# Layer 0 of a two-layer encoder trunk: inverse square roots of a head pair by one Heron step and reciprocals, with the intermediate rows in PSUM

## The chip, the cores and the metric

One core of a Trainium2 chip runs the whole step as one program. The metric is the device time of one execution in microseconds (us). TensorE (PE) multiplies matrices into PSUM, VectorE (DVE) and ScalarE (ACT) work on SBUF and PSUM, GpSimd (POOL) on SBUF, and SyncE (SP) issues nearly all DMAs. Each engine takes its instructions in the order of its own queue; semaphores hold an instruction back until what it needs is there.

## The reference

One inference step on a prompt of 512 tokens and a sample of 32. Layer 0 is an RWKV-7 time mixer, layer 1 a differential attention; each has one input projection, four heads of attention to a memory, a gate, and an output projection. What matters here are two normalizations in layer 0's mixer, both by head of 64 columns:

```python
kk = k * k_k
kk = kk / jnp.maximum(jnp.linalg.norm(kk, axis=-1, keepdims=True), 1e-12)
...
mean = jnp.mean(y, axis=-1, keepdims=True)
var = jnp.mean(jnp.square(y - mean), axis=-1, keepdims=True)
y = (y - mean) * lax.rsqrt(var + GN_EPS) * ln_w + ln_b
```

Both need an inverse square root: one per token and head of the squared norm of the keys, one of the variance of the outputs.

## The kernel before

The 512 + 32 = 544 tokens lie in one matrix. Layer 0 works through its 24 heads in 12 pairs. Three strands are woven together, in an order that a table of numbers (`PLAN`, line 49, with `FILL0` to `FILL3` ahead of the loop and `TAIL` behind it, lines 83 to 89) and a small planner in `layer0` write out:

- the main stream: projections with weight blocks of 128 columns. PE makes a block in two halves of 272 tokens, each of 24 products into one PSUM buffer `ps_g`, as the operands are split in a high and a low part (`hh`, `hl` and `whi`, `wlo`). DVE makes `wlo` of the next block (line 106 is the helper through which every instruction of PE, DVE, ACT and SP goes, so nearly all rows of the profile say L106).
- the chain of a pair: the state `SB` is carried from chunk to chunk by small products into `ps_c`, which DVE and ACT take up.
- steps of other pairs: the preparation of pairs to come (`rw_prep`, "prep"), and the end of the pair before (`rw_finish`, "fin").

PSUM is handed out in pools. The pool `psg` (line 2167) has three buffers of one bank each, given out in turn; all half products of the main stream take theirs there, and a buffer is written again only when the last reader of what was in it is done. At the end of layer 0 the output projection starts (`w_out`, line 1382). For a block of its first kind it takes two buffers at once, one for each half of the tokens, and alternates between them.

The inverse square roots of a pair are made by one call. `rw_prep` of one pair puts the 16 squared norms of each partition into the first columns of the row tile `q20` (line 669), and `rw_finish` of an earlier pair puts 10 variances behind them (line 1103). The entry "rsq" of the table (line 67, in `TAIL`, and three calls ahead of the loop) then calls `rsqrt` on all 26 columns (line 1468), which leaves the results in `r20`. `rw_finish` multiplies the pair's outputs `yt` by ten of them (line 1105), after which PE transposes `yt` into `ps_y`; `rw_prep` copies the other 16 into `rr` (line 699). There are 16 calls. In the profile both `q20` and `r20` are called `q`, and the scratch row `nt`.

`rsqrt` (line 131) is the integer estimate of an inverse square root, one Newton step and one step of higher order: eight DVE instructions, each on 128 partitions of 26 numbers in SBUF, each using the result of the one ahead of it. Other places in the kernel use it too, and are not touched.

On POOL, `rw_invert` (lines 861 and 863) makes the triangular inverses of a later pair with up to 62 small instructions, at the same time.

Of the kernel before, what the change touches and what calls it, by code (L numbers as in the profile page):

```python
# [9 lines left out]
F32 = mybir.dt.float32  # L10
F32R = mybir.dt.float32r
BF16 = mybir.dt.bfloat16
I32 = mybir.dt.int32
AF = mybir.ActivationFunctionType
ALU = mybir.AluOpType
AX = mybir.AxisListType

P = 128
# [90 lines left out]
class Trunk:  # L109
# [21 lines left out]
    def rsqrt(self, y, x, pool, tag):  # L131

        nc = self.nc
        t = pool.tile(list(y.shape), F32, tag=tag, name=tag)
        f = 0.375 ** 0.2
        self.ve.tensor_scalar(y.bitcast(I32), x.bitcast(I32), -0.5, float(0x5F3759DF), ALU.mult, ALU.add)
        self.ve.scalar_tensor_tensor(t[:], y, -0.5 * f, y, ALU.mult, ALU.mult)
        self.ve.tensor_tensor(t[:], t[:], x, ALU.mult)
        self.ve.scalar_tensor_tensor(y, t[:], 1.5 * f, y, ALU.add, ALU.mult)
        self.ve.tensor_tensor(t[:], y, y, ALU.mult)  # L140
        self.ve.tensor_tensor(t[:], t[:], x, ALU.mult)
        self.ve.scalar_tensor_tensor(t[:], t[:], -10.0 / 3.0 * f ** 2, t[:], ALU.add, ALU.mult)
        self.ve.scalar_tensor_tensor(y, t[:], 5.0 * f ** 4, y, ALU.add, ALU.mult)

    def params(self, p, name, rows, queue=None):

        t = p.tile([P, P], F32, name=name)
        r0 = 0
        for src, n in rows:
            (queue or self.se).dma_start(t[r0 : r0 + n, :], src)  # L150
            r0 += n
        return t, r0
# [1281 lines left out]
    def layer0(self, mem):  # L1434
        nc, o = self.nc, self.o
        w = self.a["rw_in"][0]
# [4 lines left out]
        with ExitStack() as ctx:  # L1441
# [23 lines left out]
            def go(kind, pr):  # L1465

                if kind == "rsq":
                    self.rsqrt(self.r20[:], self.q20[:], self.rk0, "nt")
                elif 0 <= pr < NPAIR:
                    if kind in ("inv", "back", "at"):  # L1470
                        {"inv": self.rw_invert, "back": self.rw_back, "at": self.rw_at}[kind](sts[pr])
                        return
                    if (kind, pr) not in run:
                        it = run[kind, pr] = self.rw_prep(sts[pr], rkv[pr]) if kind == "prep" else make[kind](sts[pr])
                        next(it)
                    next(run[kind, pr], None)
# [96 lines left out]
            for k, n in enumerate(FILL0):  # L1573
                go("prep", 0)
                if k == 3:
                    go("rsq", 0)
                if k == 26:
                    go("inv", 0)
                fill(n)
# [94 lines left out]
        with ExitStack() as ctx:  # L1674
# [67 lines left out]
            for i in range(5):  # L1742
                n = P if i < 4 else TS
# [493 lines left out]
```

## Time and profile before

| | |
|---|---|
| median of 3 runs | 1403.26 us (1402.6 to 1403.94) |
| the profiled execution | 1402.28 us, of which the span from the first to the last instruction is 1400.5 us |
| granted TensorE clock | 0.996 |
| PE busy | 1361.5 us of the span |
| DVE busy | 934.6 us |
| ACT busy | 828.6 us |
| POOL busy | 371.7 us |

How to read it: times are us from the start of the span unless marked ns. A row of the timeline gives start, duration, engine, line, operation, what is written and read (`out<-in`), and the shape; in brackets the idle time ahead of it and who ended it. A row of the waits gives who waited for whom, the time in total, how often, and the longest. PE counts a matmul as busy from its start to its end, though matmuls overlap: products of 272 columns start 0.125 us apart while each is shown with 0.29 us.

### The profile page before, as it was taken

What the parts mean: (1) busy time and instruction counts of PE and PEld (TensorE: products, weight loads), DVE (VectorE), ACT (ScalarE), POOL (GpSimd) and SP (SyncE); (2) the same over time, 40 slices, a digit from 0 to 9 for tenths busy, and PEclk for the clock granted to TensorE, in tenths of its full rate; (3) what the DMA queues carried; (4) which work ended last, traced back from release to release, by engine and by line L of the source; (5) the groups of instructions that cost most, each with busy time, mean ns of one, the idle gap of its engine ahead of it and who ended that gap; (6) DMA issues with size and microseconds to landing.
All of it is one profiled execution on the core that took longest, in us unless ns stands there. A gap on an engine that the chain in (4) does not pass through costs nothing.

```text
span 1400.5 us, 31939 instructions
## 1 busy us (share of the span) xinstructions
PE 1361.5 (97%) x11893; PEld 1296.7 (93%) x11893; DVE 934.6 (67%) x2345; ACT 828.6 (59%) x2304; POOL 371.7 (27%) x841
## 2 busy tenths in 40 slices
PE   8999999999999999999999999999999999999997
PEld 6988899999998998897899999999999999999997
DVE  5765777787877787676753476676467756767443
ACT  5756677767776777565543366664466546665222
POOL 2136567555865576520000040000000001001000
PEclk9999999999999999999999999999999999999999
DMA  7543222332233222342474473333333322332321
GB/s 224 155 118 80 49 57 76 84 96 62 67 82 99 61 77 73 87 131 64 121 206 118 120 218 108 92 92 93 101 92 94 104 73 84 97 106 84 91 76 72
DMA packets 264036, 139.45 MB, mean 100 GB/s; under 512 B 57721, under 2 KB 252802, under 8 KB 263882
## 3 DMA queue, kind: packets, MB, share of 16 engines
q1 hardware_dynamic: 263818, 137.41, 34.9%
q8 instruction: 94, 1.54, 0.5%
q14 instruction: 60, 0.49, 0.1%
q10 hardware_dynamic: 64, 0.02, 0.0%
HBM read 111.12 MB, written 22.91 MB: 96 GB/s over the span
## 4 chain that ended last, share of the span: by engine, by line
PE 81%; DVE 8%; ACT 3%; issue 2%; POOL 2%; DMA 2%; SPq 1%; DVEq 0%; ACTq 0%; POOLq 0%
PE ps_g L106 57%; PE ps_c L106 4%; PE ps_s L106 2%; PE ps_o L106 2%; PE ps_at L106 2%; DVE wlo L106 1%; PE ps_v L106 1%; SPq L106 1%; PE ps_mm L106 1%; PE ps_mo L106 1%; POOL tm L861 1%; PE ps_aT L106 1%; PE ps_yc L106 1%; POOL u L863 1%; PE ps_kv L106 1%
## 5 line engine op out<-in xcount | busy, mean ns | idle before, releaser
L106 PE MATMUL ps_g<-hh,whi 128*128 128x272 f32 x1808 | 541.0, 300 | 0.4 <-DVE memk L106 0.2
L106 PE MATMUL ps_g<-hh,wlo 128*128 128x272 f32 x1808 | 536.0, 297 | 1.6 <-DVE wlo L106 1.6
L106 PE MATMUL ps_g<-hl,whi 128*128 128x272 f32 x1808 | 532.1, 295 | 0.6 <-DVE hl L106 0.3
L106 PEld LDWEIGHTS ps_g<-hh,wlo 128*128 128x128 f32 x1808 | 341.7, 189 | 6.3 <-DVE wlo L106 2.3
L106 PEld LDWEIGHTS ps_g<-hh,whi 128*128 128x128 f32 x1808 | 341.9, 189 | 5.8 <-DVE og L106 0.6
L106 PEld LDWEIGHTS ps_g<-hl,whi 128*128 128x128 f32 x1808 | 341.8, 189 | 4.6 <-DVE hl L106 1.3
L106 DVE TENSOR_TENSOR wlo<-raw,whi 128x512 fp32r<-128x512 f32 x314 | 220.9, 714 | 123.0 <-ACT whi L106 119.2
L106 ACT CAST whi<-raw 128x512 fp32r<-128x512 f32 x314 | 189.1, 619 | 109.5 <-PE ps_g L106 61.4
L861 POOL TENSOR_TENSOR tm<-u,m 102x84 f32<-102x84 f32 (+23 forms) x341 | 143.7, 421 | 165.5 <-DMA m<-sc 139.7
L863 POOL TENSOR_TENSOR u<-u,tm 102x84 f32<-102x84 f32 (+23 forms) x341 | 148.3, 435 | 26.6
L106 PE MATMUL ps_g<-hi,whi 128*128 128x272 f32 x512 | 148.9, 291 | 0.0
L106 PE MATMUL ps_g<-hi,wlo 128*128 128x272 f32 x512 | 147.5, 288 | 0.5 <-DVE wlo L106 0.5
L106 PE MATMUL ps_g<-lo,whi 128*128 128x272 f32 x512 | 147.4, 288 | 0.0
L1333 POOL TENSOR_TENSOR lo<-og,hi 128x544 fp32r<-128x544 f32 x8 | 13.2, 1652 | 359.7 <-ACT hi L106 359.2
L106 PEld LDWEIGHTS ps_g<-hi,wlo 128*128 128x128 f32 x512 | 96.4, 188 | 0.8 <-DVE wlo L106 0.7
L106 PEld LDWEIGHTS ps_g<-hi,whi 128*128 128x128 f32 x512 | 96.4, 188 | 0.0
L106 PEld LDWEIGHTS ps_g<-lo,whi 128*128 128x128 f32 x512 | 96.4, 188 | 0.0
L106 ACT ACTIVATE pt<-ps_s,snm 128x128 f32<-128x128 f32 (+3 forms) x96 | 51.0, 532 | 41.7 <-DVE snm L106 41.6
L106 DVE SCALAR_TENSOR_TENSOR SB<-ps_c,dl,sd 64x64 f32<-64x64 f32 x168 | 47.4, 282 | 40.9 <-PE ps_c L106 37.7
L1754 POOL TENSOR_TENSOR hl<-hn,hh 128x544 fp32r<-128x544 f32 x8 | 12.5, 1567 | 211.3 <-ACT hh L106 211.2
L106 ACT ACTIVATE sg<-ps_g 128x272 f32<-128x272 f32 x64 | 25.3, 396 | 57.6 <-PE ps_g L106 53.0
L106 ACT COPY sv<-ps_c 64x64 f32<-64x64 f32 x192 | 39.5, 206 | 33.3 <-PE ps_c L106 31.2
(402 smaller groups left out, 2578.3 us busy)
## 6 DMA issues: line engine op xcount, KB each, us to landing
raw<-in_rw_in_dram SPq DMA_DIRECT2D x114, 256.0 KB
raw<-in_df_in_dram SPq DMA_DIRECT2D x112, 256.0 KB
raw<-in_w_out_dram SPq DMA_DIRECT2D x64, 256.0 KB
oscr<-sg SPq DMA_DIRECT2D x16, 272.0 KB
lo<-oscr SPq DMA_DIRECT2D x16, 272.0 KB
m<-sc SPq DMA_DIRECT2D x33, 128.0 KB
raw<-in_w_mem_v_dram SPq DMA_DIRECT2D x16, 256.0 KB
kh<-kh SPq DMA_DIRECT2D x24, 136.0 KB
```

What stands on the lines that cost most here:

```text
L106: return lambda *a, **k: self.trunk.tie(self, issue(*a, **k))
L861: nc.gpsimd.tensor_tensor(tm[:, :n, :wd], u3[:, :n, kx : kx + 1].to_broadcast(sh), m3[:, kx : kx + 1, kx + 1 :].to_broadcast(sh), ALU.mult)
L863: nc.gpsimd.tensor_tensor(u3[:, :n, kx + 1 :], u3[:, :n, kx + 1 :], tm[:, :n, :wd], ALU.add)
L1333: (self.nc.gpsimd if g % 2 and self.o1 else self.ve).tensor_tensor(lo[:], t, hi[:].bitcast(F32), ALU.subtract)
L1754: nc.gpsimd.tensor_tensor(self.hl[:, k, :], h[:], self.hh[:, k, :].bitcast(F32), ALU.subtract)
```

## The change

In place of `rsqrt`, the 16 calls of layer 0 use a new function, `roots`. With x in `q20` it takes an integer estimate u of the square root (not of its inverse), makes u plus x/u (twice the result of a Heron step), and combines the reciprocal of that sum with the sum over 4x into the inverse square root. The constant m balances the error. There are again eight DVE instructions, three of which are reciprocals. The tile `u` is the scratch row in SBUF; the three rows z, w and d lie in a PSUM tile that comes from the pool `psg`.

```diff
+    def roots(self):
+
+        x, out = self.q20[:], self.r20[:]
+        n = x.shape[1]
+        u = self.rk0.tile([P, n], F32, tag="nt", name="nt")[:]
+        ps = self.psg.tile([P, 512], F32, tag="g", name="ps_nt")
+        z, w, d = (ps[:, i * n : i * n + n] for i in range(3))
+        m = 3.0e-4
+        self.ve.tensor_scalar(u.bitcast(I32), x.bitcast(I32), 0.5, float(0x1FBB4F2E), ALU.mult, ALU.add)
+        self.ve.reciprocal(z, x)
+        self.ve.reciprocal(w, u)
+        self.ve.tensor_tensor(d, w, x, ALU.mult)
+        self.ve.tensor_tensor(u, d, u, ALU.add)
+        self.ve.reciprocal(w, u)
+        self.ve.scalar_tensor_tensor(u, u, 0.25 * (1.0 - m), z, ALU.mult, ALU.mult)
+        self.ve.scalar_tensor_tensor(out, w, 1.0 + m, u, ALU.mult, ALU.add)
...
                 if kind == "rsq":
-                    self.rsqrt(self.r20[:], self.q20[:], self.rk0, "nt")
+                    self.roots()
```

The instructions of the engines stand in the same order as before but for the eight of each call, and for one load of SP's queue at the turn of the layers (`cmt`, a tile of cached memory keys), which moves ahead of three others.

On DVE, in the loop over pairs, the call stands between the token shift of a later block (`rkv`) and the low half of the next weights (`wlo`), ahead of the multiplication of `yt`. Here `q_99` is `q20` and `q_100` is `r20`. Before:

```order
L106 SCALAR_TENSOR_TENSOR rkv<-raw_485,PA,rkv 128x544
L106 TENSOR_SCALAR q_100<-q_99 128x26
L106 SCALAR_TENSOR_TENSOR nt<-q_100 128x26
L106 TENSOR_TENSOR nt<-nt,q_99 128x26
L106 SCALAR_TENSOR_TENSOR q_100<-nt,q_100 128x26
L106 TENSOR_TENSOR nt<-q_100 128x26
L106 TENSOR_TENSOR nt<-nt,q_99 128x26
L106 SCALAR_TENSOR_TENSOR nt<-nt 128x26
L106 SCALAR_TENSOR_TENSOR q_100<-nt,q_100 128x26
L106 TENSOR_TENSOR wlo<-raw,whi 128x512
L106 TENSOR_TENSOR yt_1689<-yt_1689,q_100 128x640
```

And in the change:

```order
L106 SCALAR_TENSOR_TENSOR rkv<-raw_485,PA,rkv 128x544
L106 TENSOR_SCALAR nt<-q_99 128x26
L106 RECIPROCAL ps_nt<-q_99 128x26
L106 RECIPROCAL ps_nt<-nt 128x26
L106 TENSOR_TENSOR ps_nt<-ps_nt,q_99 128x26
L106 TENSOR_TENSOR nt<-ps_nt,nt 128x26
L106 RECIPROCAL ps_nt<-nt 128x26
L106 SCALAR_TENSOR_TENSOR nt<-nt,ps_nt 128x26
L106 SCALAR_TENSOR_TENSOR q_100<-ps_nt,nt 128x26
L106 TENSOR_TENSOR wlo<-raw,whi 128x512
L106 TENSOR_TENSOR yt_1691<-yt_1691,q_100 128x640
```

Nothing has moved around the call. Of its own instructions, in the old call each reads what the one ahead of it wrote; in the new one the first reciprocal reads only `q_99`.

On PE, at the start of the output projection, the last half of the last gate (`hh` and `wlo`) is followed by the first products of the output projection, where `hi0` and `lo0` are the parts of a gated branch output. The numbers are those of the buffers' tiles, and "waits" names the engine's semaphore. Before:

```order
L106 MATMUL ps_g_10621<-hh_75,wlo_10412 128x272
L106 MATMUL ps_g_10676<-hi0_9333,whi_10541 128x272 [waits DVE_49,Activation_49]
L106 MATMUL ps_g_10676<-lo0_9334,whi_10541 128x272
L106 MATMUL ps_g_10676<-hi0_9333,wlo_10542 128x272 [waits DVE_49]
L106 MATMUL ps_g_10677<-hi0_9333,whi_10541 128x272 [waits DVE_49]
L106 MATMUL ps_g_10677<-lo0_9334,whi_10541 128x272
```

And in the change:

```order
L106 MATMUL ps_g_10636<-hh_75,wlo_10427 128x272
L106 MATMUL ps_g_10692<-hi0_9346,whi_10556 128x272 [waits DVE_49,Activation_49]
L106 MATMUL ps_g_10692<-lo0_9347,whi_10556 128x272
L106 MATMUL ps_g_10692<-hi0_9346,wlo_10557 128x272
L106 MATMUL ps_g_10693<-hi0_9346,whi_10556 128x272 [waits DVE_49]
L106 MATMUL ps_g_10693<-lo0_9347,whi_10556 128x272
```

The products stand as they stood. What the first product into the second tile (`ps_g_10677`, now `ps_g_10693`) waits for is another: before it was DVE's last reading of a gate half that had been in that buffer, now it is the last instruction of the sixteenth call, whose tile `ps_nt` had the buffer in between.

Also on PE, four half products earlier, the first product of a gate's half follows the last one of the half ahead. Before:

```order
L106 MATMUL ps_g_10334<-hl_76,whi_10115 128x272
L106 MATMUL ps_g_10334<-hh_75,wlo_10116 128x272
L106 MATMUL ps_g_10413<-hh_75,whi_10282 128x272
L106 MATMUL ps_g_10413<-hl_76,whi_10282 128x272
L106 MATMUL ps_g_10413<-hh_75,wlo_10283 128x272
```

And in the change:

```order
L106 MATMUL ps_g_10348<-hl_76,whi_10129 128x272
L106 MATMUL ps_g_10348<-hh_75,wlo_10130 128x272
L106 MATMUL ps_g_10428<-hh_75,whi_10296 128x272 [waits DVE_49]
L106 MATMUL ps_g_10428<-hl_76,whi_10296 128x272
L106 MATMUL ps_g_10428<-hh_75,wlo_10297 128x272
```

With `ps_nt` of the fifteenth call in between, the tile there now comes to a buffer that was in use one half product later than the one it had before, and so the first product has a wait for DVE.

## The prediction

> **What bounds the kernel now.** I read the page first. The busy times say that TensorE hardly rests, and the chain that ended last is mostly its own work.
>
> ```profile
> PE 1361.5 (97%) x11893; PEld 1296.7 (93%) x11893; DVE 934.6 (67%) x2345; ACT 828.6 (59%) x2304; POOL 371.7 (27%) x841
> PE 81%; DVE 8%; ACT 3%; issue 2%; POOL 2%; DMA 2%; SPq 1%; DVEq 0%; ACTq 0%; POOLq 0%
> ```
>
> So VectorE (DVE) work costs time only where TensorE (PE) stands still for it. The second view is the list of waits, narrowed to PE and to layer 0's loop over head pairs (150 to 698 us):
>
> ```profile
> PE ps_y L106 <- DVE yt L106: 5.0, 10, 0.9
> PE ps_w L106 <- DVE t1b L106: 2.1, 4, 1.1
> ```
>
> The longest wait of PE there is the one that this change touches: ten times it waits to transpose `yt` (the normalized output of a pair) into `ps_y`. The third view, the timeline of DVE around one of the ten, shows why; its columns are start, duration, operation. Then PE at the same place.
>
> ```profile
> 214.40 0.17 DVE L106 TENSOR_SCALAR q<-q 128x26 int32<-128x26 int32 x1
> 214.60 0.19 DVE L106 SCALAR_TENSOR_TENSOR nt<-q 128x26 f32<-128x26 f32 x1
> 214.83 0.19 DVE L106 TENSOR_TENSOR nt<-nt,q 128x26 f32<-128x26 f32 x1
> ...
> 215.96 0.19 DVE L106 SCALAR_TENSOR_TENSOR q<-nt,q 128x26 f32<-128x26 f32 x1
> 216.06 0.73 DVE L106 TENSOR_TENSOR wlo<-raw,whi 128x512 fp32r<-128x512 f32 x1
> 216.72 0.85 DVE L106 TENSOR_TENSOR yt<-yt,q 128x640 f32<-128x640 f32 x1
> 217.50 0.57 DVE L106 SCALAR_TENSOR_TENSOR SB<-ps_c,dl,sd 64x64 f32<-64x64 f32 x2
> ```
>
> ```profile
> 217.09 0.29 PE L106 MATMUL ps_g<-hh,whi 128*128 128x272 f32 x1
> 217.72 0.41 PE L106 MATMUL ps_y<-ident,yt 128*128 128x128 f32 x2 [0.35 <-DVE yt L106]
> ```
>
> The eight `q`/`nt` rows are one call of `rsqrt`. DVE then goes without a pause through `wlo` and `yt`, and PE starts 0.15 us after `yt` ends (217.57). Every nanosecond of the call is therefore a nanosecond of PE here, up to the length of the wait. The state update `SB` stands behind it on the same queue and moves along with it. The shortest of the ten waits is
>
> ```profile
> 681.45 0.33 PE L106 MATMUL ps_y<-ident,yt 128*128 128x128 f32 x1 [0.24 <-DVE yt L106]
> ```
>
> so a saving of up to 0.24 us per call counts in full ten times. Of the other six calls, the first four have no `yt` behind them, and at two (577 and 697 us) PE does not wait for `yt`. After 698 us PE's waits are empty for over 100 us, so what is lost or won by then stays.
>
> **The call itself.** Instructions of the 16 calls, by shape (columns: count, busy us, mean ns of one, idle before):
>
> ```profile
> L106 DVE SCALAR_TENSOR_TENSOR q<-nt,q 128x26 f32<-128x26 f32 x32 | 6.5, 203 | 1.1
> L106 DVE TENSOR_TENSOR nt<-nt,q 128x26 f32<-128x26 f32 x32 | 6.0, 188 | 1.1
> L106 DVE SCALAR_TENSOR_TENSOR nt<-nt 128x26 f32<-128x26 f32 x16 | 3.7, 230 | 0.5
> L106 DVE TENSOR_SCALAR q<-q 128x26 int32<-128x26 int32 x16 | 3.1, 196 | 0.2
> L106 DVE TENSOR_TENSOR nt<-q 128x26 f32<-128x26 f32 x16 | 3.1, 191 | 0.6
> L106 DVE SCALAR_TENSOR_TENSOR nt<-q 128x26 f32<-128x26 f32 x16 | 3.0, 187 | 0.5
> ```
>
> Before: 196 + 187 + 2 x 188 + 2 x 203 + 191 + 230 = 1586 ns. Each instruction waits for the one ahead; from its end to the next start it is 35 ns (0.22 us from start to start, 187 of work). Seven such gaps are 245 ns, the call 1.83 us. Undisturbed it would be 1.73; the stretched means, 230 and 203, come from rows like these:
>
> ```profile
> 444.09 0.30 POOL L863 TENSOR_TENSOR u<-u,tm 102x54 f32<-102x54 f32 x1
> 444.12 0.31 DVE L106 SCALAR_TENSOR_TENSOR q<-nt,q 128x26 f32<-128x26 f32 x1
> ```
>
> A DVE instruction that reads two SBUF tiles and starts beside one of GpSimd (POOL) took 310 ns in place of 187.
>
> After: also eight instructions, but the first reciprocal (`z`) needs only `x`, so it doesn't wait for the one ahead. What such an instruction gains is in the timeline above: `wlo` starts at 216.06, 0.09 us before `q` ends at 216.15. The new sum is: the integer estimate 196; `z` 190 less 95 of overlap; then six that wait, each with a gap of 35: `w` 190, `d` 187, `u` 187, `w` again 190, and the last two 187 each. That is 196 + 95 + 225 + 222 + 222 + 225 + 222 + 222 = 1629 ns, or **0.20 us less per call** (0.13 from the missing wait, the rest because no instruction reads two SBUF tiles any longer, so that I take the POOL stretching as gone; if it stays, the saving is 0.10). Two prices in it are not in the trace.
>
> First, a reciprocal 26 wide. The trace has narrow ones:
>
> ```profile
> L106 DVE RECIPROCAL srs<-srs 128x2 f32<-128x2 f32 x51 | 8.4, 166 | 26.7 <-ACT pt L106 26.0
> L106 DVE RECIPROCAL mrs<-mrs 128x1 f32<-128x1 f32 x8 | 1.3, 162 | 3.1 <-ACT mp L106 3.0
> L106 DVE SCALAR_TENSOR_TENSOR fr<-tm_t,fr 128x2 f32<-128x2 f32 x2 | 0.3, 162 | 0.1
> L106 DVE SCALAR_TENSOR_TENSOR nt<-os 128x1 f32<-128x1 f32 x3 | 0.5, 153 | 0.0
> ```
>
> At two elements it takes 4 ns more than another operation of that size (166 against 162). I take 4 as a fixed surplus, which gives 190. Below, it is no surplus. Above, all of the 9 ns by which one element differs (162 against 153) recurs for each of 26: 25 x 9 = 225 ns per reciprocal, 0.68 per call. The rows speak against that, since the second element adds 4 ns (166 less 162), where other operations add 1.04 a piece (162 to 187 from 2 to 26 elements).
>
> The Trainium skill, VectorE: DVE Perf Modes, section "Walkthrough: the 8-slice pipeline in each mode", says that Reciprocal is an iterative divide with a repeat count of 8. Read as eight cycles of 0.96 GHz per element this is an estimate of 7.3 ns extra for each, 0.55 us per call, and the whole change would come out 5 us slower; the 4 ns of the second element do not agree with it.
>
> Second, a PSUM operand on DVE (seven of the eight have one).
>
> ```profile
> L106 DVE TENSOR_SCALAR q<-ps_s 128x16 f32<-128x16 f32 x12 | 2.1, 175 | 1.9 <-PE ps_s L106 1.6
> L106 DVE TENSOR_SCALAR oss<-oss 128x16 f32<-128x16 f32 x3 | 0.5, 175 | 1.6 <-ACT jk L106 1.6
> L106 DVE MEMSET ps_s<- 64x64 f32 x96 | 10.8, 112 | 19.2 <-PE ps_s L106 18.8
> L106 DVE MEMSET cum<- 128x9 f32 x12 | 0.8, 66 | 0.1
> L106 DVE SCALAR_TENSOR_TENSOR SB<-ps_c,dl,sd 64x64 f32<-64x64 f32 x168 | 47.4, 282 | 40.9 <-PE ps_c L106 37.7 <-PE ps_si L106 1.2 <-ACT mp L106 0.2
> ```
>
> The nearest pair is the first: same operation and width, PSUM or SBUF source, 175 and 175. I take nothing. The lower end is a fill: 55 elements more at 1.04 would make 66 into 123, and into PSUM it takes 112, so 11 ns less for each of seven, 0.08 per call. The upper end is `SB`: 187 + 38 x 1.04 = 227 for an SBUF operation of 64 elements, against 282, so 55 ns more for each of seven (its per-partition scalar put down to PSUM too), 0.39 per call.
>
> The Trainium skill, Perfetto Trace Analysis, section "Optimizing Scalar/DVE Operations", gives DVE about 60 ns of overhead on SBUF and 125 on PSUM, which speaks against this change. With 65 ns for each of the four instructions that read PSUM, an estimate, a call would be 0.06 longer than before and not 0.20 shorter; the pair of 175 ns does not show it.
>
> **What the PSUM tile does to PE.** `ps_nt` takes one of the three buffers that PE accumulates in, in turn. In the loop that is covered: the half products after a call find their buffers read long before (one is at the limit, below). Not at the last call. There the output projection opens two accumulations side by side, and the second gets the buffer that `ps_nt` has just been given. DVE first, then PE:
>
> ```profile
> 696.72 0.17 DVE L106 TENSOR_SCALAR q<-q 128x26 int32<-128x26 int32 x1
> ...
> 698.26 0.19 DVE L106 SCALAR_TENSOR_TENSOR q<-nt,q 128x26 f32<-128x26 f32 x1
> ```
>
> ```profile
> 697.27 0.29 PE L106 MATMUL ps_g<-hi,wlo 128*128 128x272 f32 x1
> 697.40 0.29 PE L106 MATMUL ps_g<-hi,whi 128*128 128x272 f32 x1
> ```
>
> The product of 697.40 is the first into that second buffer. It will wait for the end of the call: 698.45 as it stands, 0.10 earlier when this undisturbed call (1.73) becomes 1.63, and 0.1 for the hand-over (the 0.15 at `ps_y` includes a weight load): 698.45. Behind it on PE stands everything, so **1.05 us are lost once**. Nothing covers it, as PE has no later wait that could shrink. The limit case is the product of 677.56, whose buffer is now the one that DVE reads last at 677.56:
>
> ```profile
> 677.13 0.43 DVE L106 SCALAR_TENSOR_TENSOR sg<-sg,ps_g 128x272 f32<-128x272 f32 x1
> ```
>
> I put 0.05 on it. The other calls' shorter DVE work, and one small load on SP's queue that moves up three places at the turn of the layers, are worth nothing: no wait of PE above hangs on them.
>
> **The sum.** 10 x -0.20 + 1.05 + 0.05 = **-0.9 us**. The profiled execution took 1402.28 us with a span of 1400.5, and the median of the three runs is 1403.26 (1402.6 to 1403.94); on the median's scale the forecast is **1402.3 us**. 0.2%, about what a measurement of this kernel can tell from no change, is 2.8 us, so this is no change.
>
> **The rivals.**
> - *Slow reciprocals.* Place: the three reciprocals of each call, on DVE ahead of `yt`. Each extra ns per element costs 3 x 25 ns a call, and a call counts eleven times (ten waits and the last stall): 0.83 us. From -0.9 it passes +2.8 at 4.5 ns per element. The bound of 9 gives +6.5, 1409.8; with the 3 ns that the second element shows it is +1.6, still no change. For: a single element already costs 9 ns more than its neighbours. Against: the second element. 20%, with what lies over 4.5.
> - *PSUM operands cost DVE time.* By the `SB` row, 0.39 x 11 = +4.2, so +3.3, 1406.6; it decides against the change from 48 ns per operand. Against it the pair of equal 175 ns. 13%, about a third of it above +2.8.
> - *PSUM operands save time and the last stall is hidden.* 11 ns a piece is -0.9, and without the stall -2.9: 1400.4. For: the fill row. Against: the order in which buffers are handed out. 12%.
> - *The new call saves nothing that counts*, POOL stretches it as before: 10 x -0.10 + 1.05 + 0.05 = +0.1, 1403.4. 10%.
> - The forecast has the rest, 45%.
>
> The change does not take work away: both have eight instructions, so that the saving hangs on one wait and on POOL.
>
> **How the numbers follow.** Faster by over 0.2%: the third rival and a bit of the forecast, 14%. Slower by over 0.2%: the first, and a third of the second, 24%. In between 62%. The range reaches from 1400.0 (all of the third rival) to 1407.0 (all of the second, and slow reciprocals up to 5 ns per element), and leaves out the worst of the first.
>
> **What would show it.** Right: in the profile after, the reciprocals 26 wide near 190 ns, a call of 1.6 us from its first start to its last end, PE's ten waits for `yt` together near 3 us, and one new wait of PE at the start of the output projection of about 1 us, ended by DVE's last instruction of a call. Wrong: reciprocals over 300 ns with the waits for `yt` above 8 us; PSUM rows above 220; or PE going into the output projection without a pause.

## The result, and the profile of the changed kernel

| | before | change |
|---|---|---|
| median, 21 runs of each | 1402.72 us | 1404.86 us |
| lowest and highest | 1398.87, 1404.32 | 1402.62, 1407.23 |
| ratio, 95% interval | | 1.0016 [1.0009, 1.0023] |
| profiled execution | 1402.28 us, span 1400.5 | 1405.38 us, span 1403.5 |
| granted clock of it | 0.996 | 0.995 |

The change costs 0.16%, about 2.2 us (1.3 to 3.2 by the interval). That is less than the 0.2% called no change, but it lies on the other side of zero from the 0.9 us that were forecast as a gain, and the interval leaves zero out.

The page of the changed kernel, its busy times and the chain, hardly differs from before: the engines' totals cannot show this change.

```profile
PE 1361.5 (97%) x11893; PEld 1296.3 (92%) x11893; DVE 937.4 (67%) x2345; ACT 827.8 (59%) x2304; POOL 370.7 (26%) x841
PE 83%; DVE 8%; ACT 4%; issue 2%; DMA 1%; SPq 1%; DVEq 0%; ACTq 0%
```

PE's waits between 150 and 720 us do show it. The wait for `yt` has grown from 5.0 to 6.5 us, and there is one of 1.2 us for `q`, the result of a call, that was not there:

```profile
PE ps_y L106 <- DVE yt L106: 6.5, 10, 0.8
...
PE ps_g L106 <- DVE q L106: 1.2, 1, 1.2
```

Together they are 2.7 us, which is enough for the measured loss of 2.2. The first of the two is not known to better than about 1 us, though: e8 below leaves layer 0 as it was before, with the same instructions of DVE and POOL in the same order, and in its trace the wait for `yt` is

```profile
PE ps_y L106 <- DVE yt L106: 6.1, 10, 0.9
```

So two traces of one and the same layer 0 have 5.0 and 6.1, with mean calls of 1.83 and 1.86 us. The wait for `q` is in neither of them. The groups of DVE by shape show which instructions it is (columns: count, busy us, mean ns of one, idle before):

```profile
L106 DVE RECIPROCAL ps_nt<-nt 128x26 f32<-128x26 f32 x32 | 10.4, 324 | 1.1
L106 DVE RECIPROCAL ps_nt<-q 128x26 f32<-128x26 f32 x16 | 5.0, 313 | 0.0
L106 DVE TENSOR_SCALAR nt<-q 128x26 int32<-128x26 int32 x16 | 3.4, 213 | 0.2
L106 DVE TENSOR_TENSOR ps_nt<-ps_nt,q 128x26 f32<-128x26 f32 x16 | 3.1, 193 | 0.5
L106 DVE TENSOR_TENSOR nt<-ps_nt,nt 128x26 f32<-128x26 f32 x16 | 3.0, 186 | 0.5
L106 DVE SCALAR_TENSOR_TENSOR q<-ps_nt,nt 128x26 f32<-128x26 f32 x16 | 3.0, 185 | 0.6
L106 DVE SCALAR_TENSOR_TENSOR nt<-nt,ps_nt 128x26 f32<-128x26 f32 x16 | 2.9, 182 | 0.5
```

The reciprocals take 313 and 324 ns, where the forecast had 190. The four other rows with a PSUM operand lie between 182 and 193. The estimate ahead of them, which has no PSUM operand, takes 213, where 196 were forecast. The same call as the one shown of before, in the timeline of DVE, has the eight in their places:

```profile
213.93 0.17 DVE L106 TENSOR_SCALAR nt<-q 128x26 int32<-128x26 int32 x1
214.01 0.32 DVE L106 RECIPROCAL ps_nt<-q 128x26 f32<-128x26 f32 x1
214.36 0.32 DVE L106 RECIPROCAL ps_nt<-nt 128x26 f32<-128x26 f32 x1
214.72 0.19 DVE L106 TENSOR_TENSOR ps_nt<-ps_nt,q 128x26 f32<-128x26 f32 x1
...
215.17 0.32 DVE L106 RECIPROCAL ps_nt<-nt 128x26 f32<-128x26 f32 x1
215.53 0.18 DVE L106 SCALAR_TENSOR_TENSOR nt<-nt,ps_nt 128x26 f32<-128x26 f32 x1
215.74 0.18 DVE L106 SCALAR_TENSOR_TENSOR q<-ps_nt,nt 128x26 f32<-128x26 f32 x1
```

From 213.93 to 215.92 it is 1.99 us; the mean of the 16 calls, first start to last end, is 2.04 against 1.83 before. The first reciprocal starts 0.09 us before the end of the instruction ahead of it (214.10), as forecast. The second does not, though it needs nothing of the first; that comes back below. At the start of the output projection the timeline of PE shows the new wait:

```profile
698.98 0.29 PE L106 MATMUL ps_g<-hi,wlo 128*128 128x272 f32 x1
700.48 0.39 PE L106 MATMUL ps_g<-hi,whi 128*128 128x272 f32 x1 [1.21 <-DVE q L106]
```

The two start 1.50 us apart in place of 0.13. The last instruction of the sixteenth call ends at 700.42, and PE goes on 0.06 us later.

### The profile page after: what moved, and what is told of

The parts are those of the page before. It is cut to its first block, busy times and chain, and to the rows that moved or that the text cites. A ratio compares the mean times of both kernels' runs of the same rounds, so it can differ in the third digit from the quotient of the medians.

```text
span 1403.5 us, 31938 instructions
## 1 busy us (share of the span) xinstructions
PE 1361.5 (97%) x11893; PEld 1296.3 (92%) x11893; DVE 937.4 (67%) x2345; ACT 827.8 (59%) x2304; POOL 370.7 (26%) x841
## 4 chain that ended last, share of the span: by engine, by line
PE 83%; DVE 8%; ACT 4%; issue 2%; DMA 1%; SPq 1%; DVEq 0%; ACTq 0%
PE ps_g L106 58%; PE ps_c L106 5%; PE ps_s L106 2%; PE ps_o L106 2%; PE ps_at L106 2%; DVE wlo L106 2%; PE ps_v L106 1%; PE ps_mm L106 1%; PE ps_mo L106 1%; SPq L106 1%; PE ps_aT L106 1%; PE ps_w L106 1%; PE ps_yc L106 1%; PE ps_q L106 1%; PE ps_kv L106 1%
```

## The experiments

The theory from the trace: the loss is the reciprocals' own length (0.39 us per call, felt at the ten waits) and the one wait at the output projection (1.2 us). The rivals: PSUM makes them long; or the rows in PSUM cost time in other ways; or the saving is lost somewhere that the waits don't name. For each kernel the table gives the mean call (worked out from the timeline), PE's waits for `yt`, the wait at the output projection, the sum of both waits against before (5.0 and 0), and the measured ratio.

| kernel | call, us | waits for `yt` | wait at output | by the waits | ratio to before, 95% |
|---|---|---|---|---|---|
| before | 1.83 | 5.0 | 0 | | |
| change | 2.04 | 6.5 | 1.2 | +2.7 | 1.0016 [1.0009, 1.0023] |
| e1_rows_in_sbuf | 1.93 | 6.7 | 0 | +1.7 | 1.0005 [0.9997, 1.0014] |
| e4_last_call_sbuf | 2.03 | 6.6 | 0 | +1.6 | 1.0008 [0.9998, 1.0018] |
| e3_no_reciprocals | 1.61 | 2.0 | 0.8 | -2.2 | 0.9985 [0.9976, 0.9994] |
| e2_old_rows_in_psum | 1.80 | 4.0 | 1.0 | 0.0 | 0.9998 [0.9989, 1.0007] |
| e5_old_psum_last_sbuf | 1.81 | 4.4 | 0 | -0.6 | 0.9993 [0.9984, 1.0002] |
| e7_reciprocals_twice | 3.12 | 19.7 | 2.3 | +17.0 | 1.0155 [1.0141, 1.0168] |
| e10_z_in_own_tile | 1.84 | 3.8 | 1.0 | -0.2 | 1.0009 [0.9999, 1.0019] |
| e11_free_rows_and_last_sbuf | 1.69 | 2.9 | 0 | -2.1 | 0.9980 [0.9971, 0.9988] |
| e12_free_rows_all_sbuf | 1.67 | 2.4 | 0 | -2.6 | 0.9993 [0.9983, 1.0004] |

0.001 is 1.4 us. Runs of the kernel before were taken anew with each set of experiments, so kernels are compared by their ratios. Except in e7, what the waits add up to lies inside the measured interval or within 0.2 us of it. That is no sharp test: the sums rest on one trace for each kernel, and by e8's trace (6.1 in place of 5.0) all of them would be 1.1 us lower; most would still lie inside. e8 and e9 are not in the table; e8's time says nothing, and e9 moves the waits elsewhere.

**e1_rows_in_sbuf: is it PSUM that makes them long?** The three rows go to SBUF: z to unused columns of a tile of constants (`dv`), w and d to the output row.

```diff
-        ps = self.psg.tile([P, 512], F32, tag="g", name="ps_nt")
-        z, w, d = (ps[:, i * n : i * n + n] for i in range(3))
+        z = self.spare
+        w = d = out
...
+        self.spare = dv[:, 40:66]
```

> The new call with its three intermediate rows in SBUF, no PSUM buffer taken. Theory A (the three reciprocals cost some 130 ns each over the 190 forecast, and the PSUM buffer costs one stall at the output projection): reciprocals 26 wide stay above 300 ns, a call stays at 2.0 to 2.15 us, PE's ten waits for yt stay at 6 to 8 us, the wait of 1.2 us at the start of the output projection is gone; time 0.5 to 2.5 us above the kernel before. Rival B (PSUM as operand or target makes the reciprocals slow): reciprocals fall below 220 ns, a call below 1.75 us, waits for yt at 4 us or less, time at or below the kernel before.

Measured: 1402.69 us, ratio 1.0005. The reciprocals stay long in the groups of DVE:

```profile
L106 DVE RECIPROCAL q<-nt 128x26 f32<-128x26 f32 x32 | 9.1, 286 | 0.6
L106 DVE RECIPROCAL dv<-q 128x26 f32<-128x26 f32 x16 | 4.9, 306 | 0.0
L106 DVE SCALAR_TENSOR_TENSOR q<-q,nt 128x26 f32<-128x26 f32 x16 | 3.7, 229 | 0.6
L106 DVE TENSOR_TENSOR q<-q,q 128x26 f32<-128x26 f32 x16 | 3.6, 227 | 0.6
```

So PSUM is not what makes them long, and that rival falls. The last two rows now read two SBUF tiles, and at 227 and 229 ns they are stretched beside POOL again; with one operand in PSUM they had 185 and 193 in the change. The mean of 286 hides two kinds: the second reciprocal of a call takes 251 to 260 ns, the third 316 to 318. The second overlaps the first:

```profile
216.76 0.30 DVE L106 RECIPROCAL dv<-q 128x26 f32<-128x26 f32 x1
216.98 0.25 DVE L106 RECIPROCAL q<-nt 128x26 f32<-128x26 f32 x1
```

It starts 0.08 us before the first ends (217.06), while in the change it starts 0.03 after (214.33 to 214.36). So the call is 1.93 us, a little under what was expected. e10 follows that up.

**e4_last_call_sbuf: the wait at the output projection alone.** The change, with the rows of the sixteenth call in SBUF as in e1.

```diff
-        ps = self.psg.tile([P, 512], F32, tag="g", name="ps_nt")
-        z, w, d = (ps[:, i * n : i * n + n] for i in range(3))
+        self.calls = getattr(self, "calls", 0) + 1
+        if self.calls < 16:
+            ps = self.psg.tile([P, 512], F32, tag="g", name="ps_nt")
+            z, w, d = (ps[:, i * n : i * n + n] for i in range(3))
+        else:
+            z = self.spare
+            w = d = out
```

> The change, but the sixteenth call keeps its rows in SBUF, so that no PSUM buffer is taken just ahead of the output projection. Theory A: PE's wait for DVE there (1.2 us) is gone and nothing takes its place, the waits for yt stay near 6.5 us; about 1.4 us below the change, 0.7 to 1.5 above the kernel before. Rival C (PE would be late there anyway and the stall is made up later): the same time as the change, with another wait of about 1 us within the output projection.

Measured: 1402.96 us, ratio 1.0008. The products of the output projection follow one another every 0.13 us, and PE's waits for `yt` are as in the change. The ratio is 0.0008 or 1.1 us below the change's, which is about the 1.2 us of the wait, though the two intervals overlap.

**e3_no_reciprocals: what the forecast's price would have given.** Each reciprocal becomes a `tensor_scalar` of the same tiles that writes a constant, and the factor on z is zero: the inverse roots are left out, all waits stay.

```diff
-        self.ve.reciprocal(z, x)
-        self.ve.reciprocal(w, u)
+        self.ve.tensor_scalar(z, x, 0.0, 1.0, ALU.mult, ALU.add)
+        self.ve.tensor_scalar(w, u, 0.0, 0.016, ALU.mult, ALU.add)
...
-        self.ve.reciprocal(w, u)
-        self.ve.scalar_tensor_tensor(u, u, 0.25 * (1.0 - m), z, ALU.mult, ALU.mult)
+        self.ve.tensor_scalar(w, u, 0.0, 0.016, ALU.mult, ALU.add)
+        self.ve.scalar_tensor_tensor(u, u, 0.0, z, ALU.mult, ALU.mult)
```

> The change with each of the three reciprocals replaced by a multiply-and-add by constants of the same shape, target and waits; the inverse square roots are left out (constants take their place). Theory A: a call takes 1.6 us, the ten waits for yt come to 3 to 3.5 us, the stall at the output projection is 1.0 us, and the time is 0.5 to 1.5 us below the kernel before, which is the sum of the prediction with its price of a reciprocal. Rival B (PSUM operands): the call stays above 1.85 us and the time at or above the kernel before. Rival D (a shorter call does not come through to the end): the waits for yt fall but the time does not.

Measured: 1400.41 us, ratio 0.9985, faster than before. The stand-ins take 178 and 189 ns, the call 1.61 us against the 1.63 of the forecast's sum, and the waits of PE are

```profile
PE ps_y L106 <- DVE yt L106: 2.0, 7, 0.3
```

Waits and time came out below what was expected of this run (3 to 3.5 us, and 0.5 to 1.5 us faster), but the forecast's gain of 0.9 us lies inside the interval. Against the change the call is 0.43 us shorter and the ratio 0.0031 lower, 4.3 us or ten times that; here the two intervals do not overlap. So the forecast's chain, from the call through the waits to the time, holds when its price holds. What failed is the price.

**e2_old_rows_in_psum and e5_old_psum_last_sbuf: the PSUM tile without the new formula.** The old formula with its scratch row `t` in a tile of `psg`, except where an instruction reads two rows of it; e5 takes the sixteenth call back to SBUF (`16` for `17`).

```diff
+        self.calls = getattr(self, "calls", 0) + 1
+        s = t = self.rk0.tile(list(y.shape), F32, tag="nt", name="nt")[:]
+        if self.calls < last:
+            t = self.psg.tile([P, 512], F32, tag="g", name="ps_nt")[:, : x.shape[1]]
...
+        self.ve.tensor_tensor(s, t, x, ALU.mult)
+        self.ve.scalar_tensor_tensor(t, s, -10.0 / 3.0 * f ** 2, s, ALU.add, ALU.mult)
...
-                    self.rsqrt(self.r20[:], self.q20[:], self.rk0, "nt")
+                    self.rsqrt_ps(self.r20[:], self.q20[:], 17)
```

> The old formula (no reciprocal), its scratch row in PSUM except where an instruction reads it twice. Theory A: no DVE instruction is dearer for PSUM (rows of 26 at 180 to 190 ns), a call is 1.70 to 1.78 us where the kernel before has 1.83 (less stretching beside GpSimd), the waits for yt fall from 5.0 to about 4, and the stall at the output projection is 1.1 to 1.3 us: the two nearly cancel, 0 to +0.5 us against the kernel before. Rival B: rows above 220 ns, a call above 2 us, 2 us slower or more.

> The old formula with its scratch row in PSUM for the first fifteen calls and in SBUF for the last. Theory A: the small saving of a call (1.70 to 1.78 us against 1.83, waits for yt about 4 us) without the stall at the output projection: 0.5 to 1.5 us below the kernel before. If a PSUM buffer taken in the loop costs PE something at each call, the time is not below the kernel before.

Measured: e2 1401.84 us, ratio 0.9998; e5 1402.36 us, ratio 0.9993. In both the rows with a PSUM operand take 185 to 196 ns where they took up to 230, but for the one that still reads an SBUF row twice (231 and 207). The call is 0.02 to 0.03 us shorter, the waits for `yt` lose 0.6 to 1.0 us, and in e2 the wait at the output projection takes that back. So the rows in PSUM are stretched less and the tile costs one wait. Whether it is worth anything by itself is not shown: the waits differ from before by less than the two traces of before's layer 0 do, and by the measured times neither kernel can be told from before.

**e7_reciprocals_twice: double the suspected cost.** Each reciprocal stands twice.

```diff
         self.ve.reciprocal(z, x)
+        self.ve.reciprocal(z, x)
+        self.ve.reciprocal(w, u)
         self.ve.reciprocal(w, u)
...
         self.ve.reciprocal(w, u)
+        self.ve.reciprocal(w, u)
```

> The change with each of the three reciprocals made twice in a row (the second writes the same values). Theory A: each extra one adds 0.23 us where it need not wait and 0.36 where it does, 0.7 to 1.05 us per call, and this comes through one for one at the ten waits for yt and at the stall: waits for yt 14 to 17 us, stall 2 us, time 8 to 12 us above the change. Rival D (the calls are mostly hidden): less than 4 us above the change.

Measured: 1424.28 us, 19.4 above the change, about twice what was expected. Part of it is in the waits: a call is 1.08 us longer, and PE waits at eleven sites.

```profile
PE ps_y L106 <- DVE yt L106: 19.7, 11, 2.1
PE ps_g L106 <- DVE q L106: 2.3, 1, 2.3
```

These two account for 14.3 us more than in the change; idle times of PE over 50 ns come to 49.6 in all against 33.5, so 16.1. The two profiled executions, both at a granted clock of 0.995, are 17.6 us apart (1422.97 and 1405.38). The four runs of e7 had clocks of 0.990 to 0.995, the 21 of the change 0.994 to 0.999, and e7's longest, 1427.55 us, is the one at 0.990; the other 2 us between the medians may go with the clock. The expectation let at most 1.05 us through at ten sites and at the output projection. At eleven sites and there, 1.08 us a time would be 13.0, so the doubling costs more than that; why is not shown.

**e8_series_by_width: the disputed price by itself.** The kernel before, with a series on DVE behind its last work, where nothing else runs; the series lengthens the program, and only its rows are read.

```diff
+        for n in (1, 2, 4, 8, 16, 26, 52, 104, 208):
+            self.ve.reciprocal(b[:, :n], a[:, :n])
+            self.ve.reciprocal(a[:, :n], b[:, :n])
+            self.ve.reciprocal(c[:, :n], a[:, :n])
+            self.ve.reciprocal(a[:, :n], c[:, :n])
+            self.ve.tensor_scalar(b[:, :n], a[:, :n], 1.0, 0.0, ALU.mult, ALU.add)
...
```

Here a and b lie in SBUF (`ser`), c in PSUM (`ser_ps`).

> The kernel before, followed at its very end by a series of single DVE instructions of 1 to 208 elements, each using the result of the one ahead: reciprocals SBUF to SBUF, SBUF to PSUM and PSUM to SBUF, and multiply-and-adds by constants of the same kinds. Theory A: the multiply-and-add grows by about 1 ns per element, the reciprocal by 6 ns, the same for all three places, from a few elements on; at 1 and 2 elements the two are within 10 ns. Rival B: the reciprocal grows faster only where PSUM is target or source. Its time is longer by the series and says nothing.

Measured, in the groups by shape:

```profile
L106 DVE RECIPROCAL ser<-ser 128x208 f32<-128x208 f32 x2 | 2.9, 1454 | 0.1
...
L106 DVE RECIPROCAL ser_ps<-ser 128x208 f32<-128x208 f32 x1 | 1.5, 1461 | 0.0
...
L106 DVE RECIPROCAL ser<-ser 128x26 f32<-128x26 f32 x2 | 0.6, 316 | 0.1
L106 DVE RECIPROCAL ser<-ser 128x16 f32<-128x16 f32 x2 | 0.5, 253 | 0.1
...
L106 DVE RECIPROCAL ser<-ser 128x8 f32<-128x8 f32 x2 | 0.4, 203 | 0.1
...
L106 DVE RECIPROCAL ser<-ser 128x4 f32<-128x4 f32 x2 | 0.4, 178 | 0.1
L106 DVE RECIPROCAL ser<-ser 128x2 f32<-128x2 f32 x2 | 0.3, 166 | 0.1
L106 DVE RECIPROCAL ser<-ser 128x1 f32<-128x1 f32 x2 | 0.3, 164 | 0.1
...
L106 DVE RECIPROCAL ser_ps<-ser 128x26 f32<-128x26 f32 x1 | 0.3, 324 | 0.0
...
L106 DVE TENSOR_SCALAR ser<-ser 128x208 f32<-128x208 f32 x1 | 0.3, 268 | 0.0
...
L106 DVE TENSOR_SCALAR ser<-ser 128x26 f32<-128x26 f32 x1 | 0.2, 180 | 0.0
...
L106 DVE TENSOR_SCALAR ser<-ser 128x2 f32<-128x2 f32 x1 | 0.2, 169 | 0.0
```

From 8 elements on a reciprocal grows by 6.3 ns per element: (253 - 203) / 8, (316 - 253) / 10, (1454 - 316) / 182. Between 2 and 8 it is already about the same: (178 - 166) / 2 = 6, (203 - 178) / 4 = 6.3. PSUM as a target adds 7 to 9 ns at any width and changes nothing of that slope. Only from 1 to 2 elements is it 2 ns (164 and 166), and there it takes no longer than the `tensor_scalar` at 2 (169): such rows do not show what an element costs.

**e9_yt_before_wlo: could the wait be removed another way?** The kernel before, with the step that multiplies `yt` (an entry "fin" of the table) put straight behind the call, so that `wlo` no longer stands between.

```diff
-    [[("prep", 3, 0.11, 0.17), ("mrg", 1, 0.9, 0)], [("rsq", 0, 0, 1.5)]],
-    [[("prep", 3, 0.33, 0)], [("fin", -1, 0, 0.88)]],
+    [[("prep", 3, 0.11, 0.17), ("mrg", 1, 0.9, 0)], [("rsq", 0, 0, 1.5), ("fin", -1, 0, 0.88)]],
+    [[("prep", 3, 0.33, 0)], []],
```

> The kernel before with one entry of the order table moved: the multiplication of yt stands right behind the call on DVE, ahead of the low half of the next weights (0.7 us). Theory A (PE waits for yt because of what DVE has ahead of it): the ten waits shrink by up to 0.6 us each, from 5.0 us to under 1, and the time falls by 2 to 4 us. Against it: the low half of the weights comes 0.8 us later, and if PE then waits for wlo instead, the time stays.

Measured: 1406.17 us, ratio 1.0022 [1.0013, 1.0031]. PE no longer waits for `yt` at all, and pays more elsewhere:

```profile
PE ps_q L106 <- POOL rkk L781: 6.2, 8, 1.3
```

`rkk` is POOL's last step behind the inverses. In the kernel before it ended 0.05 to 3.4 us ahead of the PE product that reads it (1.87 at the last of the nine: 566.05 and 567.92); in e9 it is PE that comes too early, 0.05 us after its end at all nine. So POOL's strand was close behind as a second limit. (In e8's trace, with layer 0 as before, it ended 1.7 to 3.8 us ahead.) The wait for `rkk` was 0.3 us before, so the two waits together are 0.9 us more; the measured loss is 3.1 (1.8 to 4.3); the rest, and why POOL runs later in e9, where its own order is unchanged, was not followed up.

**e10_z_in_own_tile: why the second reciprocal waited.** The change with z alone moved to SBUF.

```diff
-        z, w, d = (ps[:, i * n : i * n + n] for i in range(3))
+        w, d = (ps[:, i * n : i * n + n] for i in range(1, 3))
+        z = self.spare
```

> The change with one row moved: z lies in unused columns of a constants' tile in SBUF; w and d stay in the PSUM tile. In the profile of the change the second reciprocal starts 35 ns after the end of the first (214.01 + 0.32 to 214.36), though it needs nothing of it; with the rows in SBUF, z in a tile of its own, it started 0.08 us before that end and took 255 in place of 324 ns. Theory (the two were kept apart by sharing a tile): the second reciprocal takes about 255 ns and starts before the end of the first, the call goes from 2.04 to about 1.93 us, PE's ten waits for yt from 6.5 to about 5.4 us, and the whole is 1.1 us below the change, a ratio of 1.001 to the kernel before. Rival (it was PSUM as a target that kept them apart): no overlap, the call stays at 2.04 and the time at that of the change, 1.0016.

Measured: the second reciprocal, although into PSUM still, overlaps the first, takes 257 to 270 ns, and the third 323 to 325:

```profile
214.87 0.31 DVE L106 RECIPROCAL dv<-q 128x26 f32<-128x26 f32 x1
215.10 0.27 DVE L106 RECIPROCAL ps_nt<-nt 128x26 f32<-128x26 f32 x1
215.40 0.19 DVE L106 TENSOR_TENSOR ps_nt<-ps_nt,q 128x26 f32<-128x26 f32 x1
```

From the start of the first to the start of the product it is 0.53 us in place of 0.71. The call falls to 1.84 us, by more than expected (0.18 of the 0.20 us are this overlap), and the waits for `yt` from 6.5 to 3.8. So PSUM as the target of the second does not keep them apart; what the move took away is the tile that z and w shared, in different columns. (Two PSUM tiles in a row were not tried.) The traces also record which semaphores an instruction waits for and raises. In all 16 calls of both kernels the second reciprocal waits for the same semaphore of DVE. In the change the estimate raises none and the first reciprocal raises it, so the second starts only behind the first; in e10 the estimate raises it too. The order is thus a wait that stands in the program, and not something that the engine does by itself. The time is 1403.03 us, ratio 1.0009 [0.9999, 1.0019]; that is 1 us less than the change, by intervals that overlap, where the waits say 2.9.

**e11_free_rows_and_last_sbuf and e12_free_rows_all_sbuf: what the runs point to.** z apart; the product of the sum with z written over z, so that it shares nothing with the third reciprocal but what both read; the sixteenth call without PSUM. e12 is the same with no PSUM tile in any call (`w = d = out` only).

```diff
-        ps = self.psg.tile([P, 512], F32, tag="g", name="ps_nt")
-        z, w, d = (ps[:, i * n : i * n + n] for i in range(3))
+        z = self.spare
+        w = d = out
+        self.calls = getattr(self, "calls", 0) + 1
+        if self.calls < 16:
+            ps = self.psg.tile([P, 512], F32, tag="g", name="ps_nt")
+            w, d = (ps[:, i * n : i * n + n] for i in range(2))
...
-        self.ve.scalar_tensor_tensor(u, u, 0.25 * (1.0 - m), z, ALU.mult, ALU.mult)
-        self.ve.scalar_tensor_tensor(out, w, 1.0 + m, u, ALU.mult, ALU.add)
+        self.ve.scalar_tensor_tensor(z, u, 0.25 * (1.0 - m), z, ALU.mult, ALU.mult)
+        self.ve.scalar_tensor_tensor(out, w, 1.0 + m, z, ALU.mult, ALU.add)
```

> What the runs so far point to, put together: z lies in SBUF apart from w and d; the product of the sum with z is written back over z, and so needs nothing of the third reciprocal and writes nothing that it reads; in the sixteenth call w and d lie in SBUF too, so that no product of the output projection waits for the call. Theory (what shares no tile overlaps): the product starts about 0.09 us before the third reciprocal ends, the call is 1.71 us (1.84 with z apart, less 0.035 of a gap and 0.09 of overlap), the waits for yt come to 2.6 to 3.0 us in place of 5.0 in the kernel before, the new wait at the output projection is gone: 1.2 to 2.4 us below the kernel before, ratio 0.9983 to 0.9992. Rival (the product waits for its neighbour all the same): call 1.84, ratio 0.9992 to 1.0.

> The same without any PSUM tile: w and d lie in the output row in all 16 calls. Two instructions more read two SBUF tiles, the reader of w and x and the last one, so GpSimd stretches them now and then (rows of 227 and 229 ns in place of 185 to 193 with all rows in SBUF). Theory: the call is 1.71 to 1.80 us, the waits for yt 2.6 to 4.0, no wait at the output projection: ratio 0.9983 to 0.9997. If the rows in PSUM are what pays, it is 0.9995 or more, and the kernel with the PSUM tile is clearly below it.

Measured: e11 1399.87 us against 1403.04, ratio 0.9980 [0.9971, 0.9988], 2.8 us faster than before, clear of it and a little more than expected; e12 1401.24 us, 0.9993 [0.9983, 1.0004]. In e11's timeline the product now starts 0.09 us before the third reciprocal ends (214.18):

```profile
213.86 0.32 DVE L106 RECIPROCAL ps_nt<-nt 128x26 f32<-128x26 f32 x1
214.09 0.17 DVE L106 SCALAR_TENSOR_TENSOR dv<-nt,dv 128x26 f32<-128x26 f32 x1
214.30 0.19 DVE L106 SCALAR_TENSOR_TENSOR q<-ps_nt,dv 128x26 f32<-128x26 f32 x1
```

and PE's waits for `yt` in e11, then in e12, are

```profile
PE ps_y L106 <- DVE yt L106: 2.9, 9, 0.5
```

```profile
PE ps_y L106 <- DVE yt L106: 2.4, 9, 0.3
```

By their waits the two kernels are alike, so that nothing shows a worth of the PSUM tile here. The 1.4 us between their times have no place in the trace. The granted clock may be part of it: over the timed runs its mean was 0.9965 for e11 and 0.9958 for e12, and at a clock of 0.997 the runs of e11 average 1399.9 us (six), those of e12 1400.1 (two).

## Why the prediction was wrong, point by point

- **The bound and where the time is felt: right.** The ten waits for `yt` and the output projection differ by 2.7 us, and 2.2 were measured; e8's trace leaves about 1 us open in the first of the two. By the times alone, e3 shows it: 0.43 us less per call takes 4.3 us off the whole. The call grew by 0.21 us, which would be 2.1 at ten sites if all of it reached PE; they grew by 1.5.
- **The price of a reciprocal: the step that failed.** "I take 4 as a fixed surplus, which gives 190." It is 313 and 324, 0.39 us per call more. With that put into the forecast's own sum the call is 1.63 + 0.39 = 2.02 us (measured 2.04), and ten times 0.19, the last wait of 1.05 + 0.39 and the 0.05 make +3.4 us, a little above the interval's end of 3.2. The inference behind it was that the second element adds 4 ns, so that the surplus does not recur. e8 shows why rows of 1 and 2 elements cannot tell: the second element adds 2 ns, each one behind it 6.
- **The rival of slow reciprocals is what happened.** Its turning point was 4.5 ns per element of surplus; e8 gives (316 - 180) / 26 = 5.2. By its own arithmetic that is -0.9 + 5.2 x 0.83 = +3.4 us; the measured 2.2 stays under the +2.8 that it was to pass, so that its mechanism came and its time only in part. The Trainium skill, VectorE: DVE Perf Modes, section "Walkthrough: the 8-slice pipeline in each mode", read as eight cycles per element, pointed the right way; the estimate of 7.3 ns extra that was made from it was too high, as the slope is 6.3 in all.
- **No price for a PSUM operand: right but for a few ns.** Rows that only read it take 182 to 186 ns in the change, those that write it 193 there and 193 to 195 in e2 and e5, but for the stretched ones; an SBUF row beside no other work 187 in the prediction's timeline. e8 has 7 to 9 ns more for a reciprocal into PSUM. The second rival (48 ns or more) falls. The 65 ns that the Trainium skill, Perfetto Trace Analysis, section "Optimizing Scalar/DVE Operations", would add per instruction do not show in any of these rows.
- **POOL's stretching gone: right for the rows with a PSUM operand.** 230 and 203 before, 182 to 193 in the change, 227 and 229 in e1. The estimate, all in SBUF, is not free of it: in the change it takes 171 to 180 where no POOL instruction runs and up to 285 beside one, 213 on the mean, where the forecast had 196.
- **The missing wait of z: right, and half seen.** z overlaps as forecast. That w waits for z was counted (a gap of 35 ns), but not that it need not: with z in a tile of its own it doesn't, and the product behind the two starts 0.18 us earlier (e10).
- **The wait at the output projection: right.** PE lost 1.37 us there (1.50 less 0.13), of which 0.39 is the longer call; 1.05 was forecast. e4, e5 and e11 remove it.
- **The limit case of 0.05 us: did not come.** No wait of PE for `ps_g` shows between 674 and 680 us.

## What to carry to other kernels

Price an instruction at its own width: a row of one or two elements shows the fixed part of the time, not the cost of an element, and the operation may be six times slower per element (6.3 ns here against the forecast's 1.04) without a sign of it; a row of four elements beside it would have shown it. Give rows that don't depend on each other tiles of their own, since sharing a tile can order them even in different columns; here a row apart was worth 0.18 us per call, nearly as much as the new formula was forecast to save. Before a small difference of waits is read from two traces, a second trace of the same kernel tells how far the waits go by themselves; here it was 1 us. A scratch tile from a pool that another engine accumulates in is free only while no one takes two of its buffers at once.

## What the runs showed of the hardware

- A float32 reciprocal on DVE grows by 6.3 ns per element from 8 elements on (203, 253, 316 and 1454 ns at 8, 16, 26 and 208), with the same slope from and into PSUM; from 1 to 2 elements it grows by 2 ns; a `tensor_scalar` in SBUF goes from 180 at 26 to 268 at 208, 0.5 ns per element.
- An instruction of DVE that has nothing to wait for starts 0.08 to 0.09 us before the end of the one ahead, and the overlap is real: the reciprocal that takes 324 ns in the change adds 0.18 us to the chain then, 0.36 otherwise (0.53 and 0.71 us from the first reciprocal to the product in e10 and the change).
- The granted clock of one and the same kernel differed from run to run between 0.993 and 0.999, and the time mostly went with it: the kernel before, in the first set of experiments, averaged 1402.9 us at 0.996 (seven runs), 1401.8 at 0.997 (sixteen), 1400.2 at 0.998 (three) and 1401.0 at 0.999 (three). With 11 or 12 runs of a kernel the intervals above reach 1.2 to 1.5 us to either side, with 21 runs of each 1.0, so that single differences of 1 us are not clear of noise here.
